# An unused 320-byte tile in front of the weight ring of a hybrid decoder layer

## The chip, the cores and the metric

The kernel runs on one core of one Trainium2 chip. The metric is the device time of one execution in microseconds. Before the change it is 619.34 us, the median of three runs (619.2 to 619.59). A difference of about 0.2%, 1.2 us here, is what a measurement of this kernel can tell from no change.

## The reference

One decoder layer over 512 tokens of width 1024, in float32, in two parts: a mixer and a mixture of experts. Cut to what matters:

```python
h = rms_norm(x, attn_norm)
proj = h @ w_in                                   # 1024 -> 2816 columns
q_da, k_da, v_da, rw_cols, q_mem = split(proj)
o_da  = diff_attention(q_da, k_da, v_da, ...)     # 4 heads, two softmax maps each
o_rw  = rwkv7_time_mix(rw_cols, ...)              # 4 heads, state update per token
o_mem = memory_attention(q_mem, rms_norm(mem), w_mem_kv, ...)
x = x + concatenate([o_da, o_rw, o_mem]) @ w_out
xn = rms_norm(x, ffn_norm)
# top-1 of 4 groups, then top-2 of the group's 4 experts
for e in range(16):
    y = y + gate[:, e] * ((silu(xn @ w_gate[e]) * (xn @ w_up[e])) @ w_down[e])
return x + y
```

## The kernel before

**Products.** Every large product is made of three TensorE matmuls (`mm3`, L243 to L246): each operand is split into a high part and a low part of type float32r, and the kernel adds high times high, high times low and low times high. A TensorE matmul has a stationary operand, which a weight load (LDWEIGHTS) brings into the array, and a moving operand, which streams past it column by column. While one matmul streams, the load of the next one's stationary operand runs.

**The weight ring.** `WeightStream` (L73) takes all weights from HBM in chunks of 128 partitions by 1024 float32 (4096 bytes in each partition). A chunk lands in a raw slot; ScalarE copies it to `whi` (L97) and VectorE subtracts to get `wlo` (L98). The pool `ring` (L181) holds two raw slots `raw0`, `raw1` and four pairs `whi0`/`wlo0` to `whi3`/`wlo3`. Later other tiles become raw slots (`lraw`, `eraw`, and parts of `u1`, `u2`, `f1`, `f2`, `kT`, `qT`, `r_t`, `k_t`, `gg`), and two more pairs `xhi`/`xlo` join.

**Stages, in order of time.** First the combined projection's first unit (L342 to L344, 12 to 26 us: normalized activations `hm_h`/`hm_l` move, weights are stationary, 256 columns). Then the RWKV columns (`cols_unit`, 26 to 67 us, activations move, 512 columns), the memory's keys and values (67 to 83 us: memory in `v_da` and `qT` is stationary, weights move), the queries, keys and values (`proj`, 83 to 187 us: `hm` stationary, 128 columns; weights move, 256 columns), with RWKV and attention woven in on the other engines up to 242 us. The output projection follows (L1073 to L1075, 242 to 303 us, the mixer's result in `hm` stationary), the router, and from 318 to 602 us sixteen experts: `in_product` (L1358) with the gathered tokens `xh`/`xl` stationary (128 by 96) and 512 weight columns moving, `down` (L1389) with `hh`/`hl` stationary in the same shape.

**Where tiles lie.** Tiles of a pool stand one behind another in each partition, and pools stand one behind another, left side upward in the order in which they are opened. `const`, `rc` and `wk` end at byte 11,680, and there `ring` begins. Behind it stand `bigr` and, one after the other in the same place, `biga` and `late`. The pools on the right side (`hm`, `rt`, `ex`) are placed from the other end and do not depend on `ring`. The first bytes in the built program, with the remainder modulo 512:

| tile | first byte | modulo 512 | after the change |
|---|---|---|---|
| raw0 / whi0 / wlo0, and every other ring tile | 11,680 / 15,776 / 19,872, steps of 4096 | 416 | 224 |
| v_da, qT (the memory's parts), xhi, xlo, lraw, f, u, kT | e.g. 122,272 | 416 | 224 |
| hm_h / hm_l | 196,576 / 212,960 | 480 | 480 |
| xh / xl | 222,720 / 225,792 | 0 | 0 |
| hh / hl | 199,168 / 200,704 | 0 | 0 |
| eraw | 202,240, steps of 4096 | 0 | 0 |

A slice of 128 columns of `hm` is 512 bytes wide and each further slice starts a multiple of 512 later; weight slices of 256 or 512 columns also step by multiples of 512. So the distance modulo 512 between a weight slice and an `hm` slice is the same for all of them: below, *distance* is the stationary slice's first byte minus the moving slice's, modulo 512. The `xh` and `hh` slices are 96 columns, 384 bytes, so their starts run through 0, 384, 256 and 128.

Of the kernel before, what the change touches and what calls it, by code (L numbers as in the profile page):

```python
# [10 lines left out]
F32 = mybir.dt.float32  # L11
# [9 lines left out]
P = 128  # L21
# [130 lines left out]
def hybrid_layer_kernel(ctx, tc, x, mem, positions, cols, w_in, w_kv, w_out, wa2, g2, ffn, wr, br,  # L152
# [26 lines left out]
        return pools["ps"].tile([P, 512], F32, name="pt", bufs=2)  # L179

    ring = ctx.enter_context(tc.tile_pool(name="ring", bufs=1))  # L181
    ws = WeightStream(tc)
    wv = Weave(tc)
    for i in range(4):
# [1328 lines left out]
```

## Time and profile before

| | |
|---|---|
| median of 3 runs | 619.34 us |
| the profiled execution | 619.01 us, of which 617.3 us from the first to the last instruction |
[...]
| TensorE busy (matmul) | 599.2 us, 97% |
| weight loads | 484.4 us, 78% (beside the matmuls) |
| VectorE / ScalarE / GpSimd busy | 500.5 / 415.8 / 125.5 us |

A matmul's busy time is longer than the interval between two starts, since matmuls are pipelined; what a train of matmuls costs is read from the starts of its first and last one and their number.

### The profile page before, as it was taken

What the parts mean: (1) busy time and instruction counts of PE and PEld (TensorE: products, weight loads), DVE (VectorE), ACT (ScalarE), POOL (GpSimd) and SP (SyncE); (2) the same over time, 40 slices, a digit from 0 to 9 for tenths busy, and PEclk for the clock granted to TensorE, in tenths of its full rate; (3) what the DMA queues carried; (4) which work ended last, traced back from release to release, by engine and by line L of the source; (5) the groups of instructions that cost most, each with busy time, mean ns of one, the idle gap of its engine ahead of it and who ended that gap; (6) DMA issues with size and microseconds to landing.
All of it is one profiled execution on the core that took longest, in us unless ns stands there. A gap on an engine that the chain in (4) does not pass through costs nothing.

```text
span 617.3 us, 11297 instructions
## 1 busy us (share of the span) xinstructions
PE 599.2 (97%) x4178; PEld 484.4 (78%) x4178; DVE 500.5 (81%) x899; ACT 415.8 (67%) x635; POOL 125.5 (20%) x129
## 2 busy tenths in 40 slices
PE   7999999999999999999999999999999999999992
PEld 7968899999988777989986776777777777777771
DVE  5965976799846688666488999999999999988991
ACT  6488343544458776564337788888887988888880
POOL 3901011334400232223020111111100111410001
PEclk9999999999999999999999999999999999999997
DMA  9542243322342008896999999999999999799813
GB/s 304 179 121 69 89 137 86 104 68 70 99 91 71 1 3 294 284 339 213 341 299 343 364 345 365 361 372 369 368 353 357 368 360 364 229 378 374 331 27 55
DMA packets 77504, 144.21 MB, mean 234 GB/s; under 512 B 12833, under 2 KB 30497, under 8 KB 77441
## 3 DMA queue, kind: packets, MB, share of 16 engines
q1 hardware_dynamic: 69344, 126.59, 58.5%
q0 software_dynamic: 3760, 13.24, 9.1%
q10 hardware_dynamic: 4336, 3.57, 1.9%
q8 instruction: 35, 0.57, 0.4%
q14 instruction: 29, 0.23, 0.1%
HBM read 131.72 MB, written 11.67 MB: 232 GB/s over the span
## 4 chain that ended last, share of the span: by engine, by line
PE 90%; DVE 5%; DMA 2%; ACT 1%; issue 1%; POOL 0%; POOLq 0%; DVEq 0%; ACTq 0%
PE pp L244 18%; PE pp L246 17%; PE pp L245 17%; PE py L245 5%; PE py L246 4%; PE py L244 4%; PE pp L1073 2%; DVE wlo L98 2%; PE pp L1075 2%; PE pp L1074 2%; PE pt L995 2%; PE pp L1355 2%; PE py L1211 1%; PE pc L688 1%; PE pl L1178 1%
## 5 line engine op out<-in xcount | busy, mean ns | idle before, releaser
L246 PE MATMUL pp<-whi,xl 128*96 128x512 f32 x264 | 104.1, 395 | 0.0
L245 PE MATMUL pp<-wlo,xh 128*96 128x512 f32 x264 | 103.8, 394 | 0.0
L244 PE MATMUL pp<-whi,xh 128*96 128x512 f32 x264 | 101.2, 394 | 0.8 <-ACT xh L1342 0.8
L1403 POOL DMA_INDIRECT out<-ye,sidx x16 | 23.2, 1452 | 226.4 <-DVE gidx L1305 133.8
L244 PE MATMUL pp<-whi,hm_h 128*128 128x256 f32 x224 | 64.4, 288 | 0.0
L98 DVE TENSOR_TENSOR wlo<-raw,whi 128x1024 fp32r<-128x1024 f32 x42 | 52.3, 1253 | 13.8 <-ACT whi L97 13.4
L246 PE MATMUL pp<-whi,hm_l 128*128 128x256 f32 x224 | 63.2, 282 | 0.0
L97 ACT ACTIVATE whi<-raw 128x1024 fp32r<-128x1024 f32 x42 | 44.2, 1060 | 27.7 <-PE pp L246 19.1
L245 PE MATMUL pp<-wlo,hm_h 128*128 128x256 f32 x224 | 62.4, 278 | 0.0
L244 PEld LDWEIGHTS pp<-whi,xh 128*96 128x96 f32 x264 | 42.5, 161 | 19.6 <-ACT xh L1342 1.3
L246 PEld LDWEIGHTS pp<-whi,xl 128*96 128x96 f32 x264 | 42.6, 161 | 18.4
L245 PEld LDWEIGHTS pp<-wlo,xh 128*96 128x96 f32 x264 | 42.5, 161 | 18.2
L245 PE MATMUL py<-wlo,hh 128*96 128x512 f32 x120 | 47.9, 399 | 0.0
L246 PE MATMUL py<-whi,hl 128*96 128x512 f32 x120 | 47.0, 392 | 0.0
L244 PE MATMUL py<-whi,hh 128*96 128x512 f32 x120 | 47.0, 392 | 0.0
L98 DVE TENSOR_TENSOR wlo<-lraw,whi 128x1024 fp32r<-128x1024 f32 x36 | 42.6, 1218 | 2.7 <-ACT whi L97 2.7
L98 DVE TENSOR_TENSOR wlo<-u,whi 128x1024 fp32r<-128x1024 f32 x34 | 41.6, 1252 | 3.0 <-ACT whi L97 2.9
L244 PEld LDWEIGHTS pp<-whi,hm_h 128*128 128x128 f32 x224 | 42.1, 188 | 2.0 <-issue 0.7
L246 PEld LDWEIGHTS pp<-whi,hm_l 128*128 128x128 f32 x224 | 42.2, 188 | 0.6 <-issue 0.2
L245 PEld LDWEIGHTS pp<-wlo,hm_h 128*128 128x128 f32 x224 | 42.1, 188 | 0.4 <-issue 0.2
L97 ACT ACTIVATE whi<-lraw 128x1024 fp32r<-128x1024 f32 x36 | 37.1, 1058 | 5.1 <-PE pp L246 3.6
L97 ACT ACTIVATE whi<-u 128x1024 fp32r<-128x1024 f32 x34 | 35.0, 1056 | 3.0 <-PE pp L246 2.2
(407 smaller groups left out, 1564.9 us busy)
## 6 DMA issues: line engine op xcount, KB each, us to landing
raw<-in_w_in SPq DMA_DIRECT2D x22, 512.0 KB
lraw<-in_wg SPq DMA_DIRECT2D x12, 512.0 KB
lraw<-in_wu SPq DMA_DIRECT2D x12, 512.0 KB
lraw<-in_wd SPq DMA_DIRECT2D x12, 512.0 KB
u<-in_wd SPq DMA_DIRECT2D x12, 512.0 KB
f<-in_wg SPq DMA_DIRECT2D x11, 512.0 KB
u<-in_wu SPq DMA_DIRECT2D x11, 512.0 KB
eraw<-in_wd SPq DMA_DIRECT2D x10, 512.0 KB
```

The lines of the kernel that those rows point to most:

```text
L97: nc.scalar.activation(hi, slot, AF.Copy)
L98: nc.vector.tensor_sub(lo, slot, hi.bitcast(F32))
L244: T.matmul(ps, ah, bh, start=first, stop=False)
L245: T.matmul(ps, ah, bl, start=False, stop=False)
L246: T.matmul(ps, al, bh, start=False, stop=last)
L688: paired([lambda h=h, q=q: T.matmul(pq[q][:, h * P:(h + 1) * P], bk[sr(q), ci, h], u1[sr(q), q, ci, h], start=True, stop=True) for h in ra ...
L995: T.matmul(po[:, 0:P], aws[i % 2][:, kb * P:(kb + 1) * P], qk["v"][:, kb, h * P:(h + 1) * P], start=kb == 0, stop=kb == qb)
L1073: T.matmul(o, ah, hi[:, k % 4, :], start=k == k0 and i == lead, stop=False, skip_group_check=True)
L1074: T.matmul(o, ah, lo[:, k % 4, :], start=False, stop=False, skip_group_check=True)
L1075: T.matmul(o, al, hi[:, k % 4, :], start=False, stop=k == k1, skip_group_check=True)
L1355: T.transpose(ps[:, k * CAP:(k + 1) * CAP], xg[:, (b * 4 + k) * P:(b * 4 + k + 1) * P], ident[0:CAP, 0:CAP])
L1403: G.indirect_dma_start(out, bass.IndirectOffsetOnAxis(ap=si, axis=0), ye, None, compute_op=ALU.add)
```

## The change

One tile of 80 float32 (320 bytes in each partition) is put in front of the ring's tiles. Nothing reads or writes it. Every tile of `ring`, `bigr`, `biga` and `late` starts 320 bytes later; the pools in front of `ring` and those on the right side stay.

```diff
     ring = ctx.enter_context(tc.tile_pool(name="ring", bufs=1))
+    ring.tile([P, 80], F32, name="gap")
     ws = WeightStream(tc)
     wv = Weave(tc)
```

The programs built from the two files have the same instructions in the same order on TensorE, VectorE, ScalarE, GpSimd and SyncE, with the same waits; only line numbers (one more behind L181), buffer numbers and addresses differ. The distances modulo 512 become:

| stationary <- moving | before | after |
|---|---|---|
| hm <- weights (proj, output projection) | 64 | 256 |
| weights <- hm (first unit, RWKV columns) | 448 | 256 |
| memory parts <- weights | 0 | 0 |
| xh, hh slices <- expert weights | 96, 480, 352, 224 | 288, 160, 32, 416 |

## Rows read from the trace of the kernel before

**Rows 1.** The page: span, then busy time, share and instructions of TensorE.
```profile
span 617.3 us, 11297 instructions
PE 599.2 (97%) x4178; PEld 484.4 (78%) x4178; DVE 500.5 (81%) x899; ACT 415.8 (67%) x635; POOL 125.5 (20%) x129
```
**Rows 2.** The page: the chain that ended last, by engine.
```profile
PE 90%; DVE 5%; DMA 2%; ACT 1%; issue 1%; POOL 0%; POOLq 0%; DVEq 0%; ACTq 0%
```
**Rows 3.** Windows by stage: us, busy (instructions) by engine, clock, DMA share, GB/s.
```profile
84.00:190.00 106.00, 106.00 (x988) 99.63 (x987) 81.56 (x157) 53.51 (x96) 28.15 (x16) 1.00 0.35 95
242.00:304.00 62.00, 61.90 (x529) 59.38 (x530) 39.55 (x87) 31.55 (x66) 15.62 (x14) 1.00 0.85 298
345.00:602.00 257.00, 257.00 (x1256) 183.81 (x1255) 242.54 (x333) 213.49 (x246) 35.49 (x25) 1.00 0.97 333
```
**Rows 4.** Timeline, TensorE, distance 0: start us, us, instruction.
```profile
72.09 0.28 PE L244 MATMUL pp<-whi,v_da 128*128 128x256 f32 x1
...
76.77 0.28 PE L244 MATMUL pp<-whi,v_da 128*128 128x256 f32 x1
```
**Rows 5.** Timeline, TensorE, distance 64, queries and keys.
```profile
130.09 0.28 PE L244 MATMUL pp<-whi,hm_h 128*128 128x256 f32 x1
...
135.99 0.28 PE L245 MATMUL pp<-wlo,hm_h 128*128 128x256 f32 x1
```
**Rows 6.** Timeline, TensorE, distance 64, output projection.
```profile
274.70 0.28 PE L1073 MATMUL pp<-xhi,hm_h 128*128 128x256 f32 x1
...
278.47 0.28 PE L1075 MATMUL pp<-whi,hm_l 128*128 128x256 f32 x1
```
**Rows 7.** Timeline, TensorE, distance 448, the first unit.
```profile
12.80 0.28 PE L343 MATMUL pp<-hm_l,whi 128*128 128x256 f32 x1
...
15.16 0.28 PE L342 MATMUL pp<-hm_h,whi 128*128 128x256 f32 x1
```
**Rows 8.** Timeline, TensorE, expert stage: two runs of `down`, then a piece of `in_product`.
```profile
400.60 0.39 PE L246 MATMUL py<-whi,hl 128*96 128x512 f32 x1
...
401.96 0.40 PE L246 MATMUL py<-whi,hl 128*96 128x512 f32 x1
406.41 0.40 PE L245 MATMUL pp<-wlo,xh 128*96 128x512 f32 x1
...
410.14 0.39 PE L246 MATMUL pp<-whi,xl 128*96 128x512 f32 x1
```
**Rows 9.** Tile hm_h and v_da: count, min/median/max ns, first and last start.
```profile
L244 PE MATMUL pp<-whi,hm_h x224: 276/276/681, 83.0 to 186.9; 128*128 128x256 f32 x112
L1073 PE MATMUL pp<-whi,hm_h x96: 276/281/387, 242.0 to 302.8; 128*128 128x256 f32 x96
L1073 PE MATMUL pp<-xhi,hm_h x32: 276/276/367, 274.7 to 295.7; 128*128 128x256 f32 x32
L244 PE MATMUL pp<-hm_h,whi x48: 388/392/475, 26.3 to 66.8; 128*128 128x512 f32 x48
L244 PE MATMUL pp<-whi,v_da x32: 274/283/388, 67.5 to 82.6; 128*128 128x256 f32 x32
```
**Rows 10.** The chain in order of time: one expert's transposes and the next one's.
```profile
386.69 0.66 PE pp L1355 x8
...
404.54 0.66 PE pp L1355 x8
```
**Rows 11.** Tiles eraw and lraw: the split of a weight chunk, min/median/max ns.
```profile
L97 ACT ACTIVATE whi<-eraw x25: 1043/1061/1065, 364.7 to 572.5; 128x1024 fp32r<-128x1024 f32 x25
L98 DVE TENSOR_TENSOR wlo<-eraw,whi x25: 1214/1218/1227, 367.1 to 573.7; 128x1024 fp32r<-128x1024 f32 x25
L97 ACT ACTIVATE whi<-lraw x36: 1045/1060/1064, 332.4 to 593.4; 128x1024 fp32r<-128x1024 f32 x36
L98 DVE TENSOR_TENSOR wlo<-lraw,whi x36: 1211/1218/1226, 335.3 to 595.6; 128x1024 fp32r<-128x1024 f32 x36
```

## The prediction

> **What bounds the kernel now.** I read the page's busy times and the chain first, then the stages, then single trains of matmuls in the timeline. TensorE is busy 97% of a span of 617.3 us [rows 1] and holds 90% of the chain that ended last [rows 2]. [...]
>
> The intervals are not the same for equal matmuls. All of the following load 128 columns and stream 256, back to back:
> - distance 0: 39 intervals from 72.09 to 76.77 us, 120.0 ns each [rows 4];
> - distance 64: 52 intervals from 130.09 to 135.99, 113.5 ns [rows 5];
> - distance 64 again, elsewhere: 32 intervals from 274.70 to 278.47, 117.8 ns [rows 6];
> - distance 448: 20 intervals from 12.80 to 15.16, 118.0 ns [rows 7].
>
> [...] A train keeps its level until something interrupts it, and VectorE and ScalarE are at work beside trains of both levels. The experts show the same: in `down` 6 intervals of 226.7 ns (400.60 to 401.96, distance 480) and then 6 of 231.7 (to 403.35, distance 352), in `in_product` 16 of 233.1 with all four distances, all of one shape [rows 8]; the pattern repeats from expert to expert, whose period is 17.85 us [rows 10]. I take this as the load of the next stationary operand and the stream of the moving one getting in each other's way in a manner that depends on their addresses and on the phase at which a train began.
>
> **The change, part by part.** The tile itself costs nothing: no instruction, DMA or wait is added, removed or moved, on any of the five engines. What is left is where the bytes lie.
>
> The split of the weights does not feel it. A chunk from `eraw`, at 0 modulo 512, and one from `lraw`, at 416, take 1061 and 1060 ns on ScalarE and 1218 both on VectorE, into the same `whi` and `wlo` at 416 [rows 11]. Cost: 0, and a spread of 1 ns over 192 chunks of experts would be 0.2 us. The transfers keep their sizes and 4096-byte rows; no row here sets transfers to 224 against 416. They move 333 GB/s among the experts [rows 3], ahead of use, and TensorE does not stand still there, so I take 0 with bounds of nothing either way.
>
> The projections, distance 64 to 256. There are 3 x 224 matmuls in `proj` and 3 x (96 + 32) in the output projection [rows 9]. Counted in the timeline, 607 of the first kind follow each other at under 130 ns, with a mean of 114.1, and 513 of them at 115 or less; of the second kind 344, with a mean of 115.7, and 160 of them at 115 or less. The medians say the same in another form: 276 ns of modelled duration belongs to the low level and 281 to the higher one, while distance 0 has 283 [rows 9]. No train in this program has distance 256. Bounds from the nearest rows:
> - all at 120.0, as at distance 0: 607 x 5.9 ns = 3.6 us, 344 x 4.3 ns = 1.5 us;
> - all at 117.8: 607 x 3.7 = 2.2 us, 344 x 2.1 = 0.7 us;
> - all at 113.3: 607 x 0.8 = 0.5 us, 344 x 2.4 = 0.8 us gained.
>
> The first unit, distance 448 to 256: 91 close intervals at 117.8, so +0.2 us at 120.0 and -0.4 us at 113.3. The RWKV columns, also 448 to 256: 127 close intervals of 512 columns with a mean of 229.3, between the 226.7 and 233.1 seen among the experts: -0.3 to +0.5 us.
>
> The experts: 1027 close intervals between 345 and 602 us have a mean of 230.9, against a floor of 226.7. That is an excess of 4.3 us in the window and 4.8 us over all 1152 matmuls. The four distances 96, 480, 352, 224 become 288, 160, 32, 416: four values again, 128 apart. Since the interval depends on the distance and on what the one before left behind, I expect another pattern with about the same mean: 0, with bounds of -4.8 us (all at the floor) and +2.5 us (all at the 233.1 of [rows 8]).
>
> Which end for the projections? What speaks for the upper one are the experts. If matmul and load disturbed each other only near distance 0 modulo 512, the 96-column loads at 96 and 224 should stream at the floor, and they don't: in the timeline of one expert both show intervals from 226 to 237 ns, like 352 and 480. In `down`, the runs at 480 and those at 224 settle at the floor, those at 96 and 352 do not. That looks like a period of 256, or less, rather than 512, and then 256 is distance 0 again: the 120.0 of [rows 4]. What speaks for the lower end is that 256 is as far from 0 as it can be if 512 is the period.
>
> I take the upper levels, between 117.8 and 120.0. The sum lies between 2.9 and 5.3 us for the projections with the first unit, middle 4.1; the RWKV columns add 0.1, the experts 0; some 0.2 us is hidden where VectorE ends the wait in the output projection. That makes +4.0 us on the profiled execution's own 619.0, or 623.0. The median of the runs is 0.3 us above that execution: 623.3 us.
>
> [...]
>
> **The rivals.**
> - *Faster.* 512 is the period, and at 256 every train of the projections runs at 113.3: -0.5 - 0.8 - 0.4 - 0.3 = -2.0 us. If the experts lose a third of their excess with it, -1.6 more: 619.3 - 3.6 = 615.7 us. For it: distance 64 has trains at both levels, 0 only the upper. Against it: the experts' middle distances. Its far end is 619.3 - 6.8 = 612.5.
> - *No difference.* The level is set by the phase with which a train starts, and 256 mixes the levels as 64 does now; the experts change their pattern and not their mean: 619.3 us. For it: both levels stand at the same distance [rows 5, 6]. Against it: distance 0 has settled trains at 120.0 alone. [...]
> - *Slower still*, within my own case: 120.0 everywhere and the experts at 233.1: 619.3 + 5.3 + 0.5 + 2.5 = 627.6 us.
>
> **How the numbers follow.** Slower as forecast 0.42, faster 0.33, no difference 0.25. The forecast's own range is 621.2 to 626.0. With the faster case's middle inside, the range is 614.6 to 626.0; left out are its far end and the sum of all bad ends, about 0.1 each. What can be told from no change is 0.2%, 1.2 us. The forecast case puts 0.38 beyond that and 0.04 within; the faster case 0.29 beyond and 0.04 within; the third 0.17 within and 0.04 on either side. That gives faster 0.33, same 0.25, slower 0.42.
>
> **What would show it.** In the timeline of the changed kernel the train of `proj` that starts near 130 us should step by 118 to 120 ns; 113.3 proves the first rival's part there, a mix the second. The modelled medians of the tile hm_h would go from 276 to 281 or 283. The period of an expert should stay within 0.1 us of 17.85; each 0.1 us less is 1.6 us of the time. ScalarE's and VectorE's split of a chunk must stay at 1060 and 1218 ns; if it moves, the claim that only TensorE feels the addresses is wrong. I would be wrong in kind if the time moved by more than 1% and these intervals did not.

## The result and the profile after

The changed kernel takes 623.87 us, the median of four runs (623.83 to 624.47), beside 619.47 us for the kernel before in the same comparison: a ratio of 1.007, 95% interval 1.0055 to 1.0084. It is 4.4 us slower; 623.3 was forecast. The profiled execution took 623.83 us, 4.8 us more than that of before. Below, a ratio is always to the kernel before in the same comparison, with its 95% interval behind it.

The page of the changed kernel has what answers to [rows 1, 2]: span, busy time, share and instructions by engine, and the chain that ended last.

```profile
span 622.0 us, 11297 instructions
...
PE 604.4 (97%) x4178; PEld 490.2 (79%) x4178; DVE 498.7 (80%) x899; ACT 415.7 (67%) x635; POOL 122.9 (20%) x129
...
PE 92%; DVE 3%; DMA 2%; ACT 1%; issue 1%; POOL 0%; POOLq 0%; ACTq 0%; DVEq 0%
```

The counts are the same to the instruction, VectorE and ScalarE have not grown, TensorE has: the span is 4.7 us longer and TensorE's busy time 5.2 us. The windows by stage, with the columns of [rows 3], show a clock of 1.00 in all three, as before, so the matmuls did not become slower through the clock. In the first window TensorE, busy throughout, gets through 937 matmuls where it was 988. These counts show that there is a delay and not how large it is: before, the projections ended at 187.2 us, and 46 of the 988 are short matmuls of attention and RWKV behind them. In the expert window 1254 face 1256.

```profile
84.00:190.00 106.00, 106.00 (x937) 100.03 (x936) 77.92 (x150) 49.71 (x88) 26.47 (x15) 1.00 0.33 89
242.00:304.00 62.00, 61.64 (x523) 58.38 (x524) 39.65 (x88) 31.35 (x68) 14.86 (x12) 1.00 0.82 283
345.00:602.00 257.00, 257.00 (x1254) 184.04 (x1253) 241.80 (x334) 213.68 (x245) 36.75 (x26) 1.00 0.98 339
```

The timeline of TensorE (start us, us, instruction), first and last start of four trains: first unit, memory, queries and keys, output projection.

```profile
12.35 0.28 PE L344 MATMUL pp<-hm_l,whi 128*128 128x256 f32 x1
...
14.98 0.28 PE L345 MATMUL pp<-hm_h,wlo 128*128 128x256 f32 x1
...
71.11 0.28 PE L246 MATMUL pp<-wlo,v_da 128*128 128x256 f32 x1
...
76.62 0.28 PE L247 MATMUL pp<-whi,qT 128*128 128x256 f32 x1
...
129.22 0.28 PE L246 MATMUL pp<-wlo,hm_h 128*128 128x256 f32 x1
...
143.37 0.28 PE L247 MATMUL pp<-whi,hm_l 128*128 128x256 f32 x1
...
272.60 0.28 PE L1075 MATMUL pp<-wlo,hm_h 128*128 128x256 f32 x1
...
282.67 0.28 PE L1075 MATMUL pp<-wlo,hm_h 128*128 128x256 f32 x1
```

- First unit, now distance 256: 22 intervals in 2.63 us, 119.5 ns; 118.0 in [rows 7].
- Memory, distance 0 in both kernels: 46 intervals in 5.51 us, 119.8 ns; 120.0 in [rows 4].
- Queries and keys, 64 before and 256 now: 118 intervals in 14.15 us, 119.9 ns; 113.5 in [rows 5].
- Output projection, 64 before and 256 now: 84 intervals in 10.07 us, 119.9 ns; 117.8 in [rows 6].

Distance 256 looks like distance 0. The tile rows (count, min/median/max ns, first and last start) say when each stage began and ended, against [rows 9]:

```profile
L245 PE MATMUL pp<-whi,hm_h x224: 277/283/680, 82.9 to 190.3; 128*128 128x256 f32 x112
...
L1074 PE MATMUL pp<-whi,hm_h x96: 278/283/388, 245.3 to 307.4; 128*128 128x256 f32 x96
...
L245 PE MATMUL pp<-whi,v_da x32: 274/283/388, 67.5 to 82.6; 128*128 128x256 f32 x32
```

The modelled medians of 276 and 281 ns have become 283, that of distance 0. The projections start 0.1 us earlier than before (82.9 for 83.0) and issue their last 3.4 us later (190.3 for 186.9); the output projection starts 3.3 us later and ends 4.6 us later. From there the difference stands still, as the chain shows for the transposes at the head of an expert, to be read beside [rows 10]:

```profile
355.53 0.66 PE pp L1356 x8
373.38 0.66 PE pp L1356 x8
```

The same transposes in the chain of the kernel before:
```profile
350.99 0.66 PE pp L1355 x8
```
That is 4.5 us, and the expert's period is 17.85 us in both kernels. So nearly the whole loss lies in the two projections. Counted over all close intervals (under 130 ns, or under 250 with 512 columns, between two matmuls of one stage):

| stage | matmuls | before, ns | after, ns | difference, us |
|---|---|---|---|---|
| query, key, value projections | 608 | 114.15 | 119.58 | +3.3 |
| output projection | 344 | 115.74 | 119.66 | +1.35 |
| first unit | 91 | 117.77 | 119.63 | +0.17 |
| RWKV columns, 512 wide | 127 | 229.3 | 228.4 | -0.1 |
| experts, 345 to 600 us | 1007 | 230.94 | 230.97 | 0.0 |

That is 4.7 us, what the spans of the two profiled executions differ by: with TensorE busy for 106.00 of 106.00, 61.64 of 62.00 and 257.00 of 257.00 us of the three windows, a change of the interval goes into the time. Intervals of 115 ns or less in the query, key and value projections fell from 513 to 6.

### The profile page after: what moved, and what is told of

Read it like the earlier page. It is cut to its first block, busy times and chain, and to the rows that moved or that the text cites. A ratio compares the mean times of both kernels' runs of the same rounds, so it can differ in the third digit from the quotient of the medians.

```text
span 622.0 us, 11297 instructions
## 1 busy us (share of the span) xinstructions
PE 604.4 (97%) x4178; PEld 490.2 (79%) x4178; DVE 498.7 (80%) x899; ACT 415.7 (67%) x635; POOL 122.9 (20%) x129
## 4 chain that ended last, share of the span: by engine, by line
PE 92%; DVE 3%; DMA 2%; ACT 1%; issue 1%; POOL 0%; POOLq 0%; ACTq 0%; DVEq 0%
PE pp L245 18%; PE pp L247 17%; PE pp L246 17%; PE py L246 5%; PE py L247 4%; PE py L245 4%; PE pp L1074 3%; PE pp L1076 2%; PE pp L1075 2%; PE pt L996 2%; PE pp L1356 1%; PE py L1212 1%; DVE wlo L98 1%; PE pl L1179 1%; PE pc L689 1%; PE pp L1378 1%
```

## The experiments

Theory A: the interval between two matmuls depends on the distance between the next stationary slice and the moving one, modulo 256. Rivals were a dependence on absolute addresses and a period of 512 or of 128. Each kernel but the last four differs from before in the size or the place of one unused tile alone.

**1. Distance 320 (64 plus 256).**
```diff
+    ring.tile([P, 64], F32, name="gap")
```


> The unused tile is 256 bytes: distance 320 in the projections (64 plus 256), 192 in the first unit; the experts' four distances are the same set as before. Theory A (period 256: only the distance modulo 256 counts): 320 is 64 again, the projections' trains stand at 113.3 to 117.8 ns as before, 619 to 620 us. Rival B (period 512, and the middle of it is as bad as its ends): 320 lies 64 from the middle, half way, and nothing makes it equal to 64; any mean between 113.3 and 120 ns. Rival C (the absolute start of the weights decides, and 416 modulo 512 was a good one): 160 is just another start, no reason for 113 ns trains, 620 to 624 us.

Measured: 620.19 us beside 619.67, ratio 1.0009 (0.9995 to 1.0024). The timeline of TensorE, the same train:
```profile
128.48 0.28 PE L245 MATMUL pp<-wlo,hm_h 128*128 128x256 f32 x1
...
141.85 0.28 PE L246 MATMUL pp<-whi,hm_l 128*128 128x256 f32 x1
```
118 intervals in 13.37 us, 113.3 ns. The projections' mean is 114.1 ns, as before (the expectations below put it at 114.0), and the first unit's (distance 192 for 448) 117.76. Every tile behind the ring's start had moved by 256 bytes, and the time can't be told from before: the period is 256 or a divisor of it, and not 512.

**2. Distance 128.**
```diff
+    ring.tile([P, 112], F32, name="gap")
```


> The unused tile is 448 bytes: distance 128 in the projections, the first unit at 128 as well (480 minus 352, so 384 the other way, again 128 modulo 256). Theory A: half of the period, as far from a clash as can be: all trains at 113.3 ns, 617.0 to 618.0 us, the experts as after the change (their four distances are the same set as there). Rival D (period 128): 128 is a clash like 0 and 256, trains at 120 ns, 623.5 to 624.5 us. Rival B: a mean like that of 64, 619 us.

Measured: 623.48 us, ratio 1.0065 (1.0049 to 1.0082). The timeline of TensorE:
```profile
129.75 0.27 PE L245 MATMUL pp<-wlo,hm_h 128*128 128x256 f32 x1
...
143.75 0.28 PE L246 MATMUL pp<-whi,hm_l 128*128 128x256 f32 x1
```
118 intervals in 14.00 us, 118.6 ns, and not steady: single ones lie between 113 and 123 ns, where after has 117 to 120. My 113.3 for the half period was wrong: half a period away is nearly as slow as none. The steady 120 of a period of 128 isn't there either, though the time would fit it; experiment 3 tells more on that.

**3. Distance 192.**
```diff
+    ring.tile([P, 96], F32, name="gap")
```


> The unused tile is 384 bytes: distance 192 in the projections, 64 below the period of theory A. Before the change the first unit stood at 448, which is 192 modulo 256, and its trains stepped by 117.8 ns. Theory A: the projections' trains go to 117.8, 607 x 3.7 + 344 x 2.1 ns = 2.9 us, 622 us. Rival B: 192 is 64 from the middle, mirror of 320, and gives what 320 gives.

Measured: 623.24 us, ratio 1.0054 (1.0037 to 1.007); projections 117.5 ns, output projection 116.1. The level of the projections came as expected, and it differs from the 114.1 at 64, which speaks against a period of 128. The time is 1.2 us over, and its place is elsewhere: the experts have 231.6 ns for 230.9, 0.8 us over 1152 matmuls, and the RWKV columns 233.2 for 229.3, 0.5 us. The experts' four distances are the same set as before, in another order: the set alone doesn't fix their mean.

Single trains show more than the mean. Most in the projections step by 117.8 ns here, but this one in the output projection runs at the low level (timeline of TensorE):
```profile
271.45 0.28 PE L1074 MATMUL pp<-wlo,hm_h 128*128 128x256 f32 x1
...
280.97 0.28 PE L1074 MATMUL pp<-wlo,hm_h 128*128 128x256 f32 x1
```
84 intervals in 9.52 us, 113.3 ns. So 64 and 192 have the same two levels, 113.3 and 117.8, and differ in how many trains take which: 513 of 608 intervals of the projections are at 115 or less at 64, 45 here.

**4. The same distances as after, other addresses.** The ring stays where it was; a 320-byte tile on the right side, opened ahead of `hm`, moves `hm` and the expert tiles.
```diff
+    rp = ctx.enter_context(tc.tile_pool(name="rp", bufs=1, side="right")); rp.tile([P, 80], F32, name="gap")
     hm_ctx = ExitStack()
```


> No tile in front of the ring; instead one of 320 bytes in front of the activations' pools on the other side of the memory, which move by 320 the other way. The weights start at 416 modulo 512 as before the change, all distances are those of after it (256 in the projections). Theory A: 120.0 ns trains, 623.5 to 624.3 us as after the change. Rival C (absolute start of the weights): 113 to 118 ns trains, 619.3 us.

Measured: 624.14 us, ratio 1.0072 (1.0055 to 1.0088). The tile hm_h:
```profile
L244 PE MATMUL pp<-whi,hm_h x224: 277/283/682, 83.2 to 190.5; 128*128 128x256 f32 x112
...
L1073 PE MATMUL pp<-whi,hm_h x96: 278/283/386, 245.6 to 307.6; 128*128 128x256 f32 x96
```
The medians are those of after, and so are the means (119.59 and 119.64 ns; RWKV columns 228.3; experts 230.9). The weights stand at 416 modulo 512, as before the change, and in the changed kernel `hm` stood where it did before. It is the distance that counts, and not where the weights or the activations lie. The ring's raw slots and pairs didn't move here either, so neither the transfers into them nor the split of the weights explains the slower projections.

**5. and 6. Distances 32 and 96**, on either side of 64.
```diff
+    ring.tile([P, 8], F32, name="gap")      # distance 32
+    ring.tile([P, 120], F32, name="gap")    # in the other kernel: distance 96
```


> The unused tile is 32 bytes: distance 32 in the projections, between 0 (119.6 ns mean) and 64 (114.0). Theory A': a mean in between, 115 to 119 ns, 620 to 623 us; the experts' distances become 64 and 192 modulo 256, their mean is open between 227 and 233. [...]

> The unused tile is 480 bytes: distance 96 in the projections, between 64 (114.0 ns mean) and 128 (118.6). Theory A': a mean in between, 114 to 118 ns, 619.5 to 622.5 us; the experts' distances are again 64 and 192 modulo 256, as with 32 bytes. [...]

Measured: 624.37 us, ratio 1.0065 (1.0049 to 1.0081), and 623.88 us, ratio 1.0054 (1.0041 to 1.0067). The timeline of the first:
```profile
129.59 0.28 PE L245 MATMUL pp<-wlo,hm_h 128*128 128x256 f32 x1
...
143.54 0.28 PE L246 MATMUL pp<-whi,hm_l 128*128 128x256 f32 x1
```
118.2 ns; over all projections 118.3 at 32 and 118.05 at 96. No interval is below 115, and the modelled medians of the tile hm_h in the projections are 280 to 282 ns in both kernels: with the moving slices at 448 and 384 modulo 512, for 416 before, no lower floor shows. At 32 the mean lies where it was expected, at 96 just above. Both times came out over the expected ranges, by 1.4 us each; the experts (231.7 and 231.4 ns for 230.9) and the RWKV columns (233.2 and 233.4 for 229.3) make up 1.4 us at 32 and 1.0 at 96. The second expectation has the experts' distances wrong: with 480 bytes they are 0 and 128 modulo 256 and not 64 and 192. 64 is the best of the six tried, and the kernel before stood on it:

| distance modulo 256 (`hm` stationary, 256 columns) | 0 | 32 | 64 | 96 | 128 | 192 |
|---|---|---|---|---|---|---|
| mean close interval, ns | 119.6 | 118.3 | 114.1 | 118.05 | 118.65 | 117.5 |

At 64 six executions were profiled (before, and experiments 1 and 7 to 10), with 114.1 to 114.9 ns, at 0 two (after, and experiment 4), both with 119.6; the others have one each. So 0 and 64 stand clear of each other, while the order of 32, 96 and 128 among themselves isn't shown.

**7. and 8. The experts at one distance.** Before, the 96-column slices take four distances. Here `xh`, `xl`, `hh`, `hl` get 128 columns of room for each slice of 96, so that all stand at one distance; a slot of raw weights goes for the room. A 128-byte tile makes the distance 480, without it it is 96.
```diff
-NRAW = 5
+NRAW = 4
...
-        xh = ex_p.tile([P, KC, CAP], F32R, name="xh", bufs=XB)
+        xh = ex_p.tile([P, KC, 128], F32R, name="xh", bufs=XB)[:, :, 0:CAP]
...
+    rp = ctx.enter_context(tc.tile_pool(name="rp", bufs=1, side="right", reuse_waits="tile")); rp.tile([P, 32], F32, name="gap")
```


> The kernel before, with the slices of xh, xl, hh and hl 128 columns apart instead of 96, so that all expert matmuls have one distance; a tile of 128 bytes on their side sets it to 480 (224 modulo 256). One raw slot of five makes room. In the traces so far the runs of down at 480 (before) and at 224 (unused tile of 256 bytes) settled at 226.7 and 227.1 ns, while the mean over the experts was 230.9. Theory A' (the interval depends on the distance modulo 256, and the excess in the experts comes from distances at which it doesn't settle at the floor, and from changing them): every expert matmul at 226.7 ns, 1152 x 4.2 = 4.8 us less than before, 614 to 616 us. Rival F (the experts' excess comes from the other engines and the transfers beside them): no gain, 619 to 620 us.

> The same kernel as the one for 480, without the tile of 128 bytes: the same instructions in the same order, and all expert matmuls at distance 96. Theory A': runs at 96 in down stepped by 231, 227, 229 ns before, so a mean of about 229, 1152 x 1.9 = 2.2 us less than before, 617.3 us; in any case slower than at 480. Rival F: the same time as at 480.

Measured at 480: 618.49 us beside 620.05, ratio 0.9973 (0.9959 to 0.9988); at 96: 619.57, ratio 0.9988 (0.9974 to 1.0001). The gain at 480 is 1.6 us for the 4.8 expected; at 96, where 2.2 were expected, the time can't be told from before. The mean interval from 345 to 600 us is 229.7 ns at 480 and 230.7 at 96. The chain at 480, transposes at the head of each expert:
```profile
352.67 0.66 PE pp L1355 x8
370.23 0.66 PE pp L1355 x8
388.24 0.66 PE pp L1355 x8
405.80 0.66 PE pp L1355 x8
```
Two of three experts take 17.56 us, each third 18.01: at one and the same distance, trains of 71 matmuls run at a mean of 226.7 to 226.9 ns or of 233.3. The first of these heads comes 1.7 us later than before, though the experts' first matmul does not; the timeline of the kernel before, then of this one:
```profile
319.06 0.47 PE L244 MATMUL pp<-whi,xh 128*96 128x512 f32 x1 [0.44 <-ACT xh L1342]
```
```profile
319.08 0.47 PE L244 MATMUL pp<-whi,xh 128*96 128x512 f32 x1 [0.44 <-ACT xh L1342]
...
335.57 0.63 PE L244 MATMUL pp<-whi,xh 128*96 128x512 f32 x1
...
337.70 0.63 PE L246 MATMUL pp<-whi,xl 128*96 128x512 f32 x1
```
The window 318 to 345 us at 480, then at 96:
```profile
318.00:345.00 27.00, 25.20 (x135) 17.70 (x134) 22.31 (x39) 17.90 (x22) 4.65 (x4) 0.94 0.94 317
```
```profile
318.00:345.00 27.00, 25.29 (x144) 18.05 (x144) 23.70 (x41) 18.91 (x22) 4.45 (x4) 1.00 0.92 310
```
At 480 the granted clock is 0.94 there: five intervals from 335.57 to 337.70 us take 426 ns each, where the mean among the experts is 229.7, and the 0.06 that the clock lacks is 1.6 of 27 us. Ahead of them, from 330 to 336 us, TensorE was busy for 4.64 of 6 us; before, it was 4.72, and the clock stayed. The kernel at 96 has the same four slots, passes 144 matmuls and keeps 1.00 (before: 142 and 1.00). So the 1.7 us belong to the clock of this one profiled execution, which took 619.25 us, 0.8 over its median, and a missing slot alone does not bring them.

**9. and 10. Five raw slots again, distances 480 and 64.** The room comes from `ye`, two buffers for three; in the second the tile in front has 32 bytes, which gives 64.
```diff
-        ye = ex_p.tile([CAP, D], F32, name="ye", bufs=3)
+        ye = ex_p.tile([CAP, D], F32, name="ye", bufs=2)
```


> The expert slices of 96 columns lie 128 columns apart, so that all stationary slices of the experts stand at distance 480, as in the run with four raw slots; the room comes from the third ye buffer here, and five raw slots stay. Theory A (the experts gained at 480, and the 1.7 us that they began later belonged to the missing raw slot): the experts begin within 0.3 us of before (the first L1355 transposes near 351), their period stays at 17.5 to 17.7, the mean close interval at 229.7: 616.5 to 617.5 us, ratio 0.996. Rival (the late start came from the layout, or ye with two buffers delays the scatter): the experts begin near 352.7 again, 618.3 to 618.8. In no theory do the projections change: 114.0 ns.

> As the other kernel of this job, but all stationary slices of the experts at distance 64, the one at which the projections of the kernel before run at 114.0 ns. Theory A (64 is the narrow best of the distances with weights moving, whatever the number of columns): most trains of the experts at 226.7 to 227.1, mean 228 or less: 615 to 616.5 us. Rival (which level a 512-column train takes is set by the phase at which it starts, and the distance only changes the pattern): mean 229.5 to 231, 617 to 619.5 us.

Measured at 480: 618.2 us beside 619.76, ratio 0.9979 (0.9968 to 0.999). The clock of that window is 1.00, and the first head in the chain comes at 351.72 us, 0.7 us late. That delay was there when the experts began; the timeline:
```profile
319.71 0.48 PE L244 MATMUL pp<-whi,xh 128*96 128x512 f32 x1 [0.44 <-ACT xh L1342]
```
Before, this matmul started at 319.06 us. Of the 0.65 us, 0.2 lie ahead of the projections and 0.45 within them: their mean is 114.9 ns for 114.1 at the same addresses, mainly because the train of 118 intervals near 128 us took 117.8 ns for 113.4. In that the expectation failed, which had the projections unchanged in every theory. The experts' pattern of three comes back, as theory A had it, with its period; its time did not come, and neither did the rival's start near 352.7. By their ratios, 0.9979 and 0.9973, five slots and four can't be told apart.

Measured at 64: 618.08 us, ratio 0.9977 (0.9968 to 0.9986), about 0.2% under before and not to be told from the 618.2 at 480. The timeline of TensorE, one expert's train and one near the end:
```profile
475.57 0.40 PE L246 MATMUL py<-whi,hl 128*96 128x512 f32 x1
...
491.34 0.39 PE L244 MATMUL py<-whi,hh 128*96 128x512 f32 x1
...
546.16 0.39 PE L246 MATMUL py<-whi,hl 128*96 128x512 f32 x1
...
562.26 0.39 PE L244 MATMUL py<-whi,hh 128*96 128x512 f32 x1
```
Here 69 intervals take 15.77 us, 228.6 ns, and there 16.10 us, 233.3 ns: eleven trains in a row have means of 228.3 to 228.6 ns, the next three 233.2 to 233.3. The mean from 345 to 600 us is 229.5 ns; 228 or less was theory A's, 229.5 to 231 the rival's. The rival is nearer: with 512 columns, too, one distance has two levels. What makes a train take one or the other isn't shown.

## Why the prediction was right

- *The tile itself and the split of the weights, 0.* Right: the same 11297 instructions. The tile lraw, count and min/median/max ns:
```profile
L97 ACT ACTIVATE whi<-lraw x36: 1045/1061/1063, 337.0 to 597.9; 128x1024 fp32r<-128x1024 f32 x36
L98 DVE TENSOR_TENSOR wlo<-lraw,whi x36: 1208/1216/1226, 339.9 to 600.1; 128x1024 fp32r<-128x1024 f32 x36
```
  1061 and 1216 ns stand against 1060 and 1218 of [rows 11], with the raw bytes at 224 for 416 modulo 512: ScalarE and VectorE don't feel them.
- *The projections go to the level of distance 0.* Right in kind, and at the upper end: 3.3 us of the bounds 2.2 to 3.6, 1.35 of 0.7 to 1.5, with the first unit 4.8 us. I had taken 4.1, the middle between 117.8 and 120.0, though nothing but [rows 4] was at a full period; that is 0.7 us too little and the largest error in the sum.
- *The RWKV columns, +0.1.* They gained 0.1 us. With the weights stationary and 512 columns the order of distances is another: 228.4 ns at 0, 229.3 at 192, 232.3 at 128, 233.2 at 64 and 224, 233.4 at 160.
- *The experts, 0.* Right, though the pattern changed: intervals of 228 ns or less went from 303 to 109 of a thousand, at the same mean. In part this was luck: nothing in the trace fixed the mean, and in experiment 3 the same four distances in another order cost 0.8 us.
- *0.2 us hidden in the output projection.* Hardly: the stage grew by 1.3 us for a term of 1.35.
- *The argument.* That the period is 256 "or less" was drawn from the middle distances of the experts. Experiments 1, 3 and 4 bear out 256 for the projections. What I drew from it for the other distances was wrong: I thought of a bad spot at 0 and a floor away from it, and of the six distances tried only 64 has most of its trains at the floor. So the level at 256 was inferred rightly, but from a picture that was wrong elsewhere, and that is partly luck; its chance was put at 0.42.
- *The rivals.* The first fell with its period of 512. The second, a mix of levels at 256, fell with 6 intervals of 115 ns or less where there had been 513. Its premise holds elsewhere: at 64 and at 192 a long train takes some 113.4 or 117.8 ns, and the distance alone doesn't say which.
- *113.3 ns, in the bounds and in the first rival's sum.* Long trains at 64 modulo 256 do settle there: 118 intervals in 13.37 us in experiment 1. But by the distance of their operands alone the same instructions of these shapes took a mean of 114.1 or 119.6 ns.

What stays open is the cause inside the chip. That the load and the stream get in each other's way was a guess of mine; the runs show that the interval depends on the distance (114.1 ns at 64, 119.6 at 0), and not by what. Nor does any run say why 64 is better than 32, 96 or 128, or what sets which level a train takes.

## What to carry to other kernels

Where TensorE bounds a stage, read the start-to-start interval of its back-to-back matmuls against the distance between their operands' first bytes: here it was worth 5% of the interval and 3% of the query, key and value stage, and an unrelated tile was enough to move it. Before an allocation is changed in front of such a stage, compute that distance modulo 256 before and after; after it, compare the intervals before anything else. A distance that is best for one shape isn't so for another (64 for `hm` stationary and 256 moving columns, 114.1 ns; 0 for the RWKV columns, with weights stationary and 512, 228.4 ns), and at one distance trains can take different levels (113.4 or 117.8 ns at 64), so each stage has to be measured.

## What the runs showed beside this

- With `hm` stationary and 256 columns moving, the median weight load took 192 ns at distance 0 modulo 256 and 188 at 64. The tile hm_h of the changed kernel, where before a load's median was 188 ns:
```profile
L245 PEld LDWEIGHTS pp<-whi,hm_h x224: 186/192/193, 82.8 to 190.1; 128*128 128x128 f32 x112
```
  In experiment 4 it is 192 as well; at distance 128, with matmuls nearly as slow (118.65 ns), it is 188.
- Equal distances do not give equal trains. Near 270 us, at 64 modulo 256, a train stepped by 117.8 ns before [rows 6] and by 113.5 in experiment 1; in experiment 9 the projections had a mean of 114.9 ns and in experiment 10, with the same addresses up to there, 114.1. That alone is 0.5 us between two executions.
